# A batched weight gradient in bf16 on one core: five plain row pairs ahead of 27 combined ones, one set of sums packed into three PSUM banks, nine closing sums on GpSimd

## The chip, the core and the metric

The kernel runs on one core of a Trainium2 chip. The metric is the device time of one execution in microseconds. The kernel before takes 162.29 us, the median of three runs (162.11 to 162.46). All times inside an execution are microseconds from the start of the profiled span.

## What is computed

```python
# input: 16 x 512 x 1024 f32, grad_output: 16 x 512 x 768 f32
grad_weight = np.einsum('bmk,bmn->kn', input, grad_output)   # 1024 x 768 f32
```

Batch and row are summed over together, so this is one product X^T G with X of 8192 x 1024 and G of 8192 x 768. The products are done in bf16 with f32 sums.

## The kernel before

**Tiles.** The 8192 rows are taken as 32 pairs of 128 rows. `LOADS` (line 12) names the kind of each pair, in the order in which they are loaded: "s" is a plain pair, "P" a combined one. The output is cut into halves of K and of N, which gives four blocks: A (left K, left N), B (left K, right N), C (right K, left N) and D (right K, right N). A half of K is four groups of 128 columns, numbered q = 0 to 3. One product on TensorE is 128 rows of X by one q, times 384 columns of G.

A plain pair gives each block its two products per q: 2 x 4 x 4 = 32 products. A combined pair is treated as a two by two block matrix (its two rows by the two halves), of which seven products instead of eight are formed, as in Strassen's method: 7 x 4 = 28 products. Some of the seven work on the loaded data, others on sums of halves. VectorE makes these sums beforehand in six instructions a pair, three on X (`sum_x`, lines 179 to 187) and three on G (`sum_g`, lines 189 to 197). The seven products go to the streams A, B, C and to four more, 1, 5, 6 and 7 (`operands`, line 224). D gets products of plain pairs alone.

**Sums.** There are 32 running sums (a stream and a q), each 128 x 384 in f32, and eight PSUM banks. So most sums come and go: a bank is opened for one, gets some products, and is evicted into SBUF (`acc` for A to D, `macc` for 1, 5, 6, 7). There are two ways to take a sum up again. Either ScalarE first copies the stored part back into the bank and the products add onto it (`fill`, line 265, copy on line 274), and then the eviction is a plain copy (line 327 on ScalarE, line 329 on VectorE). Or the bank starts empty and VectorE adds bank and stored part when it evicts (line 331). The four sums of A stay in four banks of their own, 7, 3, 4 and 1, until the end; the other sums rotate through banks 0, 2, 5 and 6.

At the end the streams are put together (`close`, lines 301 to 321): 6 and 7 first get what they share (`SHARED`, line 253), 5 is closed by two subtractions (lines 307 and 309), and A, B, C and D get their partner added on VectorE (line 312). Each finished piece of the output is stored at once (line 320), the first three in two halves, nearly all on SyncE's queue.

**Order.** The order of the work on TensorE, VectorE and ScalarE is written out by hand in `PLAN` (lines 22 to 77), a list of tokens that the loop on line 336 turns into instructions. Each engine works through its own in this order. `A1@4.1` is one product for A, q = 1, in a newly opened bank 4, `A1.2` two more into the bank that is open. `f` fills a bank on ScalarE, `c` evicts on ScalarE and `v` on VectorE. `g0.6` to `g2.6` and `x0.6` to `x2.6` are the six sums of pair 6, and `r0` to `r4` round pieces of the first operands to bf16. The plan has 924 products; the last seven, of B3, are done in a 256-column and a 128-column piece each, as that sum lies in two banks there.

**Loads.** The first X and half of the first G come in f32 over the queues of SyncE and ScalarE and are rounded by VectorE and ScalarE (`round_by`, line 199). All the rest is loaded by GpSimd's queue, which converts to bf16 on the way (lines 152, 153, 157 and 159), one G and one X transfer a pair, in the order of `LOADS`. Each goes into one of 14 buffers. Until the first operands are there, TensorE runs four warm-up products (`WARMUP`, line 80): two of 512 columns in bf16 and two in f32.

Of the kernel before, what the change touches and what calls it, by code (L numbers as in the profile page):

```python
# [11 lines left out]
LOADS = "ssssssPPPPPPPPPPPPPPPPPPPPPPPPPs"  # L12

PLAN = (
    "A0@7.1 A3@3.1 A1@4.1 C3@5.1 C2@0.1 C1@2.1 r0 cC3 C0@6.1 vC2 A2@1.1 cC1 D0@5.1 vC0 B0@0.1 cD0 D1@2.1 "
    "r1 r3 B3@6.1 r2 D3@5.2 vB0 r4 A1.1 A2.1 cD1 vB3 A3.1 B1@0.2 cD3 B2@2.2 vB1 D2@6.2 cB2 C0@5.1 C1@0.1 "
    "vD2 A0.1 fD0@2 A2.1 vC0 A3.1 fD1@6 A1.1 D0.2 vC1 C2@5.2 cD0 D1.2 vC2 C3@0.2 cD1 B0@2.2 vC3 B3@5.3 "
    "fB1@6 vB0 A0.2 fB2@0 vB3 B1.2 fC0@2 B2.2 cB1 C1@5.2 vB2 C0.2 fD2@6 A3.1 vC1 D3@0.2 cC0 D2.2 fC2@5 "
    "vD3 C3@2.1 A1.1 cD2 A2.1 vC3 C2.1 B0@0.1 D1@6.1 vC2 D0@2.1 vB0 fD2@5 A3.2 vD1 A1.2 fB0@0 D2.2 vD0 "
    "B1@6.2 cD2 B0.2 vB1 B2@2.2 cB0 B3@5.2 vB2 C0@6.2 fC1@0 A2.2 vB3 fC2@2 C1.2 vC0 C3@5.2 cC1 C2.2 vC3 "
    "fD0@6 A0.2 D1@0.4 vC2 D3@5.4 vD1 D0.4 vD3 C3@2.2 vD0 B3@5.2 C0@0.2 vC3 fC1@6 A3.2 vB3 fB2@2 A0.2 vC0 "
    "C1.2 fD2@5 B2.2 cC1 D2.2 vB2 C2@0.2 cD2 B0@6.2 vC2 fB1@2 A1.4 vB0 fC1@0 B1.4 C2@5.2 cB1 D2@6.2 vC2 "  # L30
    "C1.2 fD0@2 A2.4 vD2 fD3@5 vC1 fC3@6 D0.2 D3.2 vD0 C3.2 cD3 C0@0.2 vC3 B2@2.4 vC0 fB3@6 B0@5.4 vB2 "
    "fD1@0 B3.4 fC0@2 vB0 A3.1 g0.6 fB1@5 A3.3 vB3 A0.2 g1.6 A0.2 fC1@6 D1.1 g2.6 D1.3 A2.2 vD1 A1.3 x0.6 "
    "fC2@0 C0.3 C1.1 x1.6 C1.2 cC0 C2.1 x2.6 C2.2 cC1 C3@2.1 g0.7 C3.2 cC2 B1.3 fD0@6 vC3 D2@0.2 g1.7 cB1 "
    "D0.2 vD2 fD3@2 A2.1 A3.1 A0.1 g2.7 cD0 10@5.1 D3.2 c10 x0.7 11@0.2 cD3 12@6.2 v11 13@5.2 c12 50@2.1 "
    "x1.7 50.1 c13 51@0.2 x2.7 52@6.2 c50 g0.8 53@5.2 c51 70@2.2 v52 c53 A2.1 g1.8 A3.1 fB3@0 72@6.2 v70 "
    "73@5.2 c72 g2.8 B3.2 v73 63@2.2 cB3 B2@6.1 x0.8 B2.1 fC1@5 A1.2 v63 A0.2 71@0.1 x1.8 71.2 vB2 62@2.3 "
    "c71 x2.8 C1.2 c62 g0.9 60@6.3 cC1 61@2.1 g1.9 61.2 fB0@0 v60 10@5.2 c61 g2.9 B0.3 v10 fC3@6 C2@2.2 "
    "cB0 x0.9 C2.1 C3.3 fC0@5 vC2 A2.2 f52@0 C0.1 x1.9 cC3 C0.2 A3.1 x2.9 A3.1 cC0 12@2.1 g0.10 12.1 52.2 "
    "f63@5 v12 B1@6.3 c52 g1.10 63.2 f13@2 vB1 11@0.2 c63 A0.1 g2.10 13.2 v11 72@5.2 c13 x0.10 A1.2 f51@0 "
    "53@6.2 v72 A0.1 f70@2 A3.1 51.1 x1.10 f50@5 51.2 v53 70.3 c51 x2.10 50.2 f73@6 g0.11 50.1 B3@0.3 c70 "  # L40
    "v50 73.2 fB2@2 g1.11 73.1 vB3 A2.1 f10@5 B2.2 c73 g2.11 B2.1 10.1 x0.11 10.2 cB2 C1@0.3 c10 x1.11 "
    "62@6.2 f71@2 vC1 A3.1 A1.1 f61@5 A0.1 x2.11 71.2 f60@0 g0.12 71.1 61.3 v62 c71 60.1 g1.12 60.2 c61 "
    "B0@2.1 g2.12 fB1@6 B0.2 v60 11@5.2 vB0 B1.2 fC0@0 A2.1 x0.12 A2.1 cB1 A0.1 C0.3 fC2@2 v11 A3.1 fC3@6 "
    "A1.1 x1.12 C2.3 cC0 x2.12 13@5.2 f53@0 g0.13 13.1 C3.3 cC2 v13 53.2 f52@2 g1.13 53.1 vC3 12@5.3 c53 "
    "g2.13 52.3 f72@6 v12 63@0.2 x0.13 c52 63.1 72.3 f62@5 v63 A2.1 f51@2 A1.1 x1.13 62.2 c72 51.1 x2.13 "
    "51.2 f50@0 v62 73@6.3 c51 g0.14 50.3 f70@5 v73 A3.1 fB2@2 A0.1 70.1 g1.14 c50 70.2 g2.14 B3@6.3 c70 "
    "B2.1 x0.14 B2.2 10@5.3 vB3 cB2 C1@0.1 x1.14 C1.2 f60@6 v10 11@2.3 x2.14 60.2 f61@5 g0.15 60.1 A1.1 "
    "61.3 c60 vC1 A0.1 g1.15 71@6.3 c61 v11 B0@0.1 fB1@5 g2.15 B0.2 v71 A2.2 fC2@2 A3.1 x0.15 A3.1 f52@6 "
    "B1.3 vB0 C2.2 cB1 x1.15 C2.1 52.2 cC2 x2.15 52.1 C0@0.1 fC3@5 g0.16 C0.2 A1.1 c52 A0.1 vC0 C3.3 "
    "f12@2 g1.16 13@6.3 vC3 12.2 g2.16 f62@5 12.1 v13 53@0.3 c12 x0.16 62.3 f72@6 A1.1 v53 63@2.3 c62 "  # L50
    "x1.16 f50@0 72.4 v63 f51@5 50.1 g0.17 50.2 c72 70@2.1 x2.16 70.2 c50 g1.17 51.3 v70 73@6.2 g2.17 c51 "
    "73.1 B2@0.1 x0.17 fB3@2 B2.2 A2.2 fC1@5 v73 B3.3 x1.17 C1.3 vB2 cB3 10@6.2 x2.17 cC1 10.1 71@0.1 "
    "g0.18 f11@2 71.2 A3.2 v10 f60@5 11.1 g1.18 11.2 v71 60.3 c11 g2.18 61@6.3 c60 x0.18 A0.3 fC0@2 v61 "
    "B1@0.3 fB0@5 x1.18 C0.3 fC2@6 vB1 B0.2 cC0 x2.18 B0.1 C2.1 g0.19 f12@0 C2.2 C3@2.3 cB0 vC2 12.2 "
    "f62@5 g1.19 12.1 vC3 A1.2 c12 53@6.1 g2.19 53.2 f52@2 x0.19 13@0.4 v53 A3.2 52.1 x1.19 f72@6 52.3 "
    "v13 62.2 x2.19 c52 62.2 g0.20 73@0.3 c62 g1.20 63@2.4 f51@5 v73 72.1 g2.20 72.2 fC1@0 v63 51.3 c72 "
    "x0.20 A2.3 c51 70@2.1 x1.20 70.3 f71@5 x2.20 50@6.4 v70 C1.1 g0.21 C1.2 fB2@2 A0.2 v50 cC1 B2.2 "
    "g1.21 B2.2 fB3@6 g2.21 A1.2 cB2 B3.4 x0.21 71.3 cB3 B0@0.2 x1.21 c71 B0.1 10@6.2 x2.21 10.2 vB0 "
    "C2@2.2 g0.22 C2.1 f61@0 A3.2 vC2 11@5.3 g1.22 11.1 f60@2 61.4 v10 g2.22 60.4 v11 c61 x0.22 C0@6.4 "
    "f53@0 c60 12@5.1 x1.22 12.3 vC0 B1@2.2 x2.22 B1.2 g0.23 C3@6.4 v12 53.2 g1.23 53.2 vB1 A1.2 c53 vC3 "  # L60
    "52@5.3 f73@2 g2.23 13@0.2 x0.23 13.2 A2.3 v52 A0.1 x1.23 A0.2 f51@5 v13 A3.2 51.1 x2.23 51.2 g0.24 "
    "51.1 73.3 c51 g1.24 73.1 C1@6.1 g2.24 C1.2 c73 63@5.4 vC1 f72@2 70@0.1 x0.24 f71@6 70.2 72.5 v63 v70 "
    "f62@5 A1.2 x1.24 c72 71.2 g0.25 71.2 f50@0 62.1 x2.24 fB2@2 62.2 g1.25 62.2 c71 B2.1 g2.25 B2.3 c62 "
    "50.4 vB2 B0@6.1 x0.25 f10@2 B0.3 c50 C2@5.1 x1.25 C2.3 f11@0 vB0 10.2 x2.25 10.2 g0.26 11.4 c10 vC2 "
    "B3@6.2 f60@2 g1.26 B3.2 c11 g2.26 B3.1 60.4 vB3 fB1@0 61@5.2 fC0@6 x0.26 61.2 c60 B1.4 v61 12@2.1 "
    "x1.26 fC3@5 12.3 vB1 C0.2 g0.27 f53@0 C0.2 x2.26 C3.2 cC0 g1.27 C3.2 v12 53.3 cC3 g2.27 53.1 52@6.4 "
    "v53 A2.1 x0.27 f51@0 A2.3 v52 A3.3 x1.27 A3.1 f70@6 A0.2 x2.27 A0.2 g0.28 A1.3 13@2.1 g1.28 13.2 "
    "g2.28 13.1 C1@5.4 v13 51.4 f73@2 vC1 70.1 x0.28 f63@5 70.3 c51 73.1 x1.28 73.3 c70 x2.28 73.1 63.2 "
    "c73 g0.29 63.3 f72@2 50@0.1 g1.29 50.2 c63 g2.29 50.1 71@6.4 v50 f62@5 72.4 fB0@0 v71 62.1 x0.29 "
    "f11@6 62.3 c72 B0.1 x1.29 B0.3 c62 x2.29 11.4 fB2@2 vB0 fC2@5 B2.1 g0.30 B2.4 f10@0 v11 C2.4 vB2 "  # L70
    "f11@6 10.1 g1.30 f12@2 10.3 vC2 A2.1 g2.30 A2.2 c10 x0.30 12.4 f13@5 f10@0 x1.30 11.1 13.3 c12 v11 "
    "10.1 A3.1 f61@2 x2.30 A3.2 v13 f62@6 A1.3 v10 f63@5 61.5 f60@0 62.2 v61 60.5 v62 f71@2 A2.2 f72@6 "
    "v60 A3.2 A1.2 vA2 f70@0 A0.5 vA3 vA1 70.3 vA0 63.2 v70 f50@1 71.2 72.2 fC0@3 v63 50.2 f73@0 v71 C0.6 "
    "f51@4 v72 fC1@5 v50 51.3 f52@2 fC2@7 C1.5 vC0 fD0@6 v51 fB0@1 52.4 fD1@3 B0.4 vC1 fB1@4 C2.3 v52 "
    "fD2@5 B1.7 vB0 fB2@2 vC2 73.2 vB1 B2.3 v73 f53@1 D0.2 D1.2 fC3@4 vB2 53.4 vD0 C3.6 vD1 v53 fD3@0 "
    "fB3@2+7 D2.2 D3.2 vC3 B3.7 vD2 vD3 vB3 "
).split()


WARMUP = [("b", 512), ("f", 512), ("f", 512), ("b", 512)]  # L80
PAIRS_HELD = 14
SUMS_HELD = 10

MERGED = 2


@with_exitstack
def kernel(
# [6 lines left out]
    nc = tc.nc  # L95
# [155 lines left out]


    SHARED = {"A": "1", "B": "5", "C": "7", "D": "1", "6": "1", "7": "6"}

    done = {(p, q): 0 for p in streams for q in range(Q)}
    fresh = {(p, q): True for p in streams for q in range(Q)}
    closed = set()
    opened = {}
    used = {7}
    stores = [0]  # L260

    def bank(b):
        return psum.tile([P, 512], f32, name=f"bank{b}")

    def fill(p, q, b, b2):
        assert (p, q) not in opened and not fresh[p, q] and b in used
        src = sum_of(p, q)
        if b2 is None:
            parts = [(bank(b), 0, NH)]
        else:  # L270
            assert b2 in used
            parts = [(bank(b), 0, 256), (bank(b2), 256, NH)]
        for tile_, c0, c1 in parts:
            nc.scalar.copy(out=tile_[:, 0 : c1 - c0], in_=src[:, c0:c1])  # L274
        opened[p, q] = (parts, True)

    def multiply(p, q, b, n):
        first = (p, q) not in opened
        if first:
            opened[p, q] = ([(bank(b), 0, NH)], False)  # L280
            used.add(b)
        parts, carried = opened[p, q]
        for tile_, c0, c1 in parts:
            for j in range(n):
                at = done[p, q] + j
                stat, mov = operands(p, streams[p][at], q)
                nc.tensor.matmul(  # L287
                    tile_[:, 0 : c1 - c0],
                    stat,
# [7 lines left out]
    def close(engine, p, q):  # L297
# [34 lines left out]
        if final:  # L332
            closed.add((p, q))
# [51 lines left out]
```

## Time and profile before

The profiled execution:

| what | value |
|---|---|
| time of the profiled execution | 162.31 us |
| its span | 160.5 us |
| granted TensorE clock, mean | 1.00 |
| read from HBM, written to HBM | 58.72 MB, 3.15 MB |
| GpSimd's load queue (q0) | 9360 packets, 28.64 MB, 90.2% of 16 DMA engines |
| median from issue to landing, X and G loads of a pair | 16.9 and 16.7 us |
| last load issued by GpSimd, last X landed | 125.6, 142.7 |
| first and last product start | 5.19, 156.64 |
| products of line 287, instructions | 631 on loaded data, 300 on sums |

The page gives busy time of each engine (PE is TensorE, PEld its weight loads, DVE VectorE, ACT ScalarE, POOL GpSimd, SP SyncE), the span in 40 slices with the busy share in tenths, the chain of work that ended last, and groups of instructions of one line and shape with busy time, the mean duration of one, and the idle time of the engine before them with what ended it. Instructions of one engine overlap by their fill and drain, so the mean duration of one is longer than the step from one to the next; where a step is spoken of, it is taken from the start times in the trace.

### The profile page before, as it was taken

What the parts mean: (1) busy time and instruction counts of PE and PEld (TensorE: products, weight loads), DVE (VectorE), ACT (ScalarE), POOL (GpSimd) and SP (SyncE); (2) the same over time, 40 slices, a digit from 0 to 9 for tenths busy, and PEclk for the clock granted to TensorE, in tenths of its full rate; (3) what the DMA queues carried; (4) which work ended last, traced back from release to release, by engine and by line L of the source; (5) the groups of instructions that cost most, each with busy time, mean ns of one, the idle gap of its engine ahead of it and who ended that gap; (6) DMA issues with size and microseconds to landing.
All of it is one profiled execution on the core that took longest, in us unless ns stands there. A gap on an engine that the chain in (4) does not pass through costs nothing.

```text
span 160.5 us, 2776 instructions
## 1 busy us (share of the span) xinstructions
PE 155.3 (97%) x937; PEld 91.9 (57%) x937; DVE 142.7 (89%) x323; ACT 112.8 (70%) x253; POOL 34.8 (22%) x69
## 2 busy tenths in 40 slices
PE   8899999999999999999999999999999999999990
PEld 3355556556556656655655655665665665556560
DVE  0788986989999999999989998998899998989992
ACT  3779737749888999968777786534777368877730
POOL 7452222122221222222122222212222100000000
PEclk9999999999999999999999999999999999999999
DMA  5999999999999999999999999999999999924385
GB/s 176 295 213 213 210 216 213 213 213 212 213 212 212 213 213 214 210 214 213 215 214 213 213 212 212 213 212 214 213 210 213 215 212 214 212 43 157 137 294 196
DMA packets 12830, 33.40 MB, mean 208 GB/s; under 512 B 1424, under 2 KB 4624, under 8 KB 12816
## 3 DMA queue, kind: packets, MB, share of 16 engines
q0 software_dynamic: 9360, 28.64, 90.2%
q1 hardware_dynamic: 3024, 3.47, 6.3%
q10 hardware_dynamic: 432, 1.11, 1.8%
q8 instruction: 7, 0.11, 0.3%
q14 instruction: 7, 0.06, 0.1%
HBM read 58.72 MB, written 3.15 MB: 385 GB/s over the span
## 4 chain that ended last, share of the span: by engine, by line
DMA 48%; PE 44%; DVE 2%; issue 2%; POOL 1%; DVEq 0%; POOLq 0%
DMA xp<-in_input_dram 48%; PE bank L287 44%; POOL gp L157 1%; DVE acc L312 1%; DVE xe L183 0%; POOL xp L159 0%; DVE acc L331 0%; DVE macc L331 0%; DVEq L380 0%; DVE xe L185 0%; POOLq L153 0%; POOLq L369 0%; POOLq L152 0%
## 5 line engine op out<-in xcount | busy, mean ns | idle before, releaser
L287 PE MATMUL bank<-gp,xp 128*128 128x384 bf16 (+2 forms) x631 | 109.8, 324 | 0.6 <-DVE xp L201 0.6
L287 PEld LDWEIGHTS <-xp 128*128 128x128 bf16 x631 | 61.1, 98 | 42.5 <-DVE xp L201 1.3
L287 PE MATMUL bank<-ge,xe 128*128 128x384 bf16 x300 | 56.2, 326 | 0.1
L274 ACT COPY bank<-macc 128x384 f32<-128x384 f32 x71 | 33.6, 484 | 13.2 <-DVE macc L331 5.6
L287 PEld LDWEIGHTS <-xe 128*128 128x128 bf16 x300 | 29.3, 98 | 19.9 <-issue 0.6
L274 ACT COPY bank<-acc 128x384 f32<-128x384 f32 (+1 forms) x70 | 32.3, 479 | 9.1 <-DVE acc L329 5.5
L327 ACT COPY macc<-bank 128x384 f32<-128x384 f32 x61 | 28.6, 479 | 9.5 <-PE bank L287 8.1
L331 DVE TENSOR_TENSOR acc<-bank,acc 128x384 f32<-128x384 f32 x54 | 28.7, 552 | 2.8 <-PE bank L287 1.2
L153 POOL DMA_DIRECT2D xp<-in_input_dram x30 | 16.0, 532 | 53.3 <-DMA xp<-in_input_dram 28.0
L327 ACT COPY acc<-bank 128x384 f32<-128x384 f32 x45 | 21.4, 480 | 6.5 <-PE bank L287 6.0
L152 POOL DMA_DIRECT2D gp<-in_grad_output_dram x30 | 16.0, 533 | 37.1 <-DMA gp<-in_grad_output_dram 15.0
L331 DVE TENSOR_TENSOR macc<-bank,macc 128x384 f32<-128x384 f32 x41 | 22.5, 551 | 0.5 <-PE bank L287 0.2
L183 DVE TENSOR_TENSOR xe<-xp 128x1024 bf16<-128x1024 bf16 x25 | 17.1, 683 | 1.2 <-DMA xp<-in_input_dram 1.2
L329 DVE COPY acc<-bank 128x384 f32<-128x384 f32 x24 | 13.1, 553 | 3.0 <-PE bank L287 2.4
L193 DVE TENSOR_TENSOR ge<-gp 128x768 bf16<-128x768 bf16 x25 | 13.8, 550 | 0.0
L187 DVE TENSOR_TENSOR xp<-xp,xe 128x512 bf16<-128x512 bf16 x25 | 10.5, 419 | 0.4
L185 DVE TENSOR_TENSOR xe<-xe,xp 128x512 bf16<-128x512 bf16 x25 | 10.5, 418 | 0.3
L197 DVE TENSOR_TENSOR gp<-ge,gp 128x384 bf16<-128x384 bf16 x25 | 8.8, 352 | 0.3
L195 DVE TENSOR_TENSOR ge<-gp,ge 128x384 bf16<-128x384 bf16 x25 | 8.7, 350 | 0.2
L312 DVE TENSOR_TENSOR acc<-bank,macc 128x384 f32<-128x384 f32 (+2 forms) x17 | 8.0, 522 | 0.0
L329 DVE COPY macc<-bank 128x384 f32<-128x384 f32 x14 | 7.6, 552 | 0.4 <-PE bank L287 0.4
L201 DVE CAST gp<-gf 128x192 bf16<-128x192 f32 (+1 forms) x2 | 0.7, 360 | 4.9 <-DMA gf<-in_grad_output_dram 4.9
(17 smaller groups left out, 21.6 us busy)
## 6 DMA issues: line engine op xcount, KB each, us to landing
xp<-in_input_dram POOLq DMA_DIRECT2D x30, 512.0 KB, 16.9
gp<-in_grad_output_dram POOLq DMA_DIRECT2D x30, 384.0 KB, 16.7
out_dram<-acc SPq DMA_DIRECT2D x12, 192.0 KB, 1.9
xf<-in_input_dram ACTq DMA_DIRECT2D x2, 512.0 KB, 5.0
gp<-in_grad_output_dram POOLq DMA_DIRECT2D x3, 192.0 KB, 6.6
out_dram<-acc SPq DMA_DIRECT2D x6, 96.0 KB, 1.7
xp<-in_input_dram POOLq DMA_DIRECT2D x2, 256.0 KB, 8.0
gf<-in_grad_output_dram SPq DMA_DIRECT2D x2, 192.0 KB, 4.2
```

Of the source, the lines that this page charges most:

```text
L152: nc.gpsimd.dma_start(out=gp, in_=G[rows, :].rearrange("(p m) n -> p m n", m=2))
L153: nc.gpsimd.dma_start(out=xp, in_=X[rows, :].rearrange("(p m) k -> p m k", m=2))
L183: nc.vector.tensor_sub(out=xe[:, 0:2, :], in0=x[:, 1::-1, :], in1=x[:, 3::-2, :])
L185: nc.vector.tensor_sub(out=xe[:, 2, :], in0=xe[:, 0, :], in1=x[:, 0, :])
L187: nc.vector.tensor_add(out=x[:, 1, :], in0=x[:, 2, :], in1=xe[:, 2, :])
L193: nc.vector.tensor_add(out=ge[:, 0:2, :], in0=g[:, 0:2, :], in1=g[:, 1::2, :])
L274: nc.scalar.copy(out=tile_[:, 0 : c1 - c0], in_=src[:, c0:c1])
L287: nc.tensor.matmul(tile_[:, 0 : c1 - c0], stat, mov[:, c0:c1], start=first and j == 0, stop=True, skip_group_check=True,)
L312: nc.vector.tensor_add(out=dst[:, c0:c1], in0=b, in1=sum_of(SHARED[p], q)[:, c0:c1])
L327: nc.scalar.copy(out=dst, in_=b)
L329: nc.vector.tensor_copy(out=dst, in_=b)
L331: nc.vector.tensor_add(out=dst, in0=b, in1=dst)
```

## The change

Seven things are changed together.

- `LOADS`: the first five pairs are plain and the other 27 combined. Before, six were plain at the start and one at the end. So there are 916 products.
- A's four sums lie packed in three banks, 5, 6 and 7. The sums of q = 0 and 3 lie whole in bank 5 and bank 7; those of q = 1 and 2 lie across two banks, 128 columns in one and 256 in the other, so that each of their products is done in two pieces, each with its own weight load. Five banks, 0 to 4, rotate for the other streams.
- D, which ends with the plain pairs, is folded into C by an addition and into 7 by a subtraction when one of their banks is evicted (token `k`, on VectorE). At the end D is 5 less the finished 7, without an addition of its own.
- A may be evicted, and B and C may be closed, by a ScalarE copy, and GpSimd then adds the shared part in SBUF (`add_shared`). Token `q` adds and stores (seven times), token `p` adds beforehand, so that the last eviction is a plain copy or an addition (twice).
- `PLAN` is written anew.
- The warm-up is one bf16 product of 512 columns and 32 of 128 columns.
- The first four stores go out in halves (`HALVED`), and the last two, of B0 and B1, use ScalarE's queue (suffix `a`).

```diff
-LOADS = "ssssssPPPPPPPPPPPPPPPPPPPPPPPPPs"
+LOADS = "sssssPPPPPPPPPPPPPPPPPPPPPPPPPPP"
 PLAN = (
-    "A0@7.1 A3@3.1 A1@4.1 C3@5.1 C2@0.1 C1@2.1 r0 cC3 C0@6.1 vC2 A2@1.1 cC1 D0@5.1 vC0 B0@0.1 cD0 D1@2.1 "
...
-    "fD2@5 B1.7 vB0 fB2@2 vC2 73.2 vB1 B2.3 v73 f53@1 D0.2 D1.2 fC3@4 vB2 53.4 vD0 C3.6 vD1 v53 fD3@0 "
-    "fB3@2+7 D2.2 D3.2 vC3 B3.7 vD2 vD3 vB3 "
+    "A0@R.1 A1@R.1 C1@0.1 C0@1.1 C3@2.1 cC1 C2@3.1 r0 A2@R.1 cC0 vC3 D1@4.1 B0@0.1 cC2 A3@R.1 vD1 B1@1.1 "
...
+    "51.2 pC0 fB3@0 51.1 71.1 C1.1 v50 C1.1 fB0@5 C1.1 A3.2 qC3 fB2@1 A3.2 v71 cC1 A3.1 B3.2 f52@4 vA3 B3.2 "
+    "qC1 fB1@6 B3.1 v51 C0@2.2 cB3 52.2 B2.2 vC0 qB3 B2.2 B0.1 v52 B0.1 cB2 B0.3 qB2 B1.2 vB0a B1.2 vB1a "
 ).split()
-WARMUP = [("b", 512), ("f", 512), ("f", 512), ("b", 512)]
+WARMUP = [("b", 512)] + 32 * [("b", 128)]
+HALVED = 4
-    SHARED = {"A": "1", "B": "5", "C": "7", "D": "1", "6": "1", "7": "6"}
+    SHARED = {"A": "1", "B": "5", "C": "7", "6": "1", "7": "6"}
+    def resident_parts(q):
+        if not resident:
+            resident.update({b: bank(b) for b in (5, 6, 7)})
+        a, b, c = (resident[i] for i in (5, 6, 7))
+        return [
+            [(a, 0, 0, NH)],
+            [(a, NH, 0, 128), (b, 0, 128, NH)],
+            [(b, 256, 0, 256), (c, 0, 256, NH)],
+            [(c, 128, 0, NH)],
+        ][q]
+        for tile_, at, c0, c1 in parts:
+            b = tile_[:, at : at + c1 - c0]
+            to = dst[:, c0:c1]
+            if engine == "c":
+                nc.scalar.copy(out=to, in_=b)
+            elif engine == "k":
+                d = sum_of("D", q)[:, c0:c1]
+                (nc.vector.tensor_add if p == "C" else nc.vector.tensor_sub)(out=to, in0=b, in1=d)
+            elif final and p == "5":
+                nc.vector.tensor_sub(out=to, in0=b, in1=sum_of("6", q)[:, c0:c1])
+                d = sum_of("D", q)[:, c0:c1]
+                nc.vector.tensor_sub(out=d, in0=b, in1=sum_of("7", q)[:, c0:c1])
+                store("D", q, c0, c1, queue)
+    def add_shared(p, q, prepare, queue):
+        dst = sum_of(p, q)
+        nc.gpsimd.tensor_add(out=dst, in0=dst, in1=sum_of(SHARED[p], q))
+        if prepare:
+            prepared.add((p, q))
+        else:
+            closed.add((p, q))
+            store(p, q, 0, NH, queue)
```

## The prediction

> **What bounds the kernel now.** I read the page from the top: busy shares, then the slices, then the chain, then the groups of instructions.
>
> ```profile
> PE 155.3 (97%) x937; PEld 91.9 (57%) x937; DVE 142.7 (89%) x323; ACT 112.8 (70%) x253; POOL 34.8 (22%) x69
> ...
> DMA  5999999999999999999999999999999999924385
> ...
> DMA xp<-in_input_dram 48%; PE bank L287 44%; POOL gp L157 1%; DVE acc L312 1%; DVE xe L183 0%; POOL xp L159 0%; DVE acc L331 0%; DVE macc L331 0%; DVEq L380 0%; DVE xe L185 0%; POOLq L153 0%; POOLq L369 0%; POOLq L152 0%
> ```
>
> Two things run at their limit side by side. TensorE is busy for 97%, and the loads fill the DMA engines up to slice 35 of 40, about 140 us; the chain is shared between them, 48 to 44. VectorE (89%) is next, ScalarE (70%) has room. Is TensorE really full where it is "busy"? The table by stretch says so, and shows how the two evicting engines stand there (columns: stretch, its length, then busy time and instructions of PE, PEld, DVE, ACT, POOL, then clock, DMA share, GB/s):
>
> ```profile
> 40.00:50.00 10.00, 10.00 (x64) 6.03 (x62) 9.86 (x24) 8.60 (x21) 2.65 (x5) 1.00 1.06 212
> 50.00:60.00 10.00, 10.00 (x63) 6.00 (x62) 9.92 (x25) 9.25 (x22) 2.12 (x4) 1.00 1.07 212
> ...
> 100.00:110.00 10.00, 10.00 (x64) 6.05 (x62) 9.88 (x24) 4.37 (x10) 2.38 (x5) 1.00 1.07 213
> ```
>
> TensorE takes some 62 products in 10 us at the full clock, and the start times of the trace give a step of 0.1625 us for 384 columns, 0.109 for 256, 0.056 for 128. VectorE works 99% of 40 to 60 us and TensorE loses nothing by it: a planned order can run an evicting engine full.
>
> So the path is: first product at 5.19 us (it waits for the rounded first operands), 917 whole products and 7 in two pieces: 917 x 0.1625 + 7 x (0.109 + 0.056) = 150.17, and 0.16 for the last to drain: 155.52. TensorE ends at 156.86, so it stood for 1.3 in all (0.5 in the first 2.6 us of products, 0.3 at 14 to 17, 0.3 at 84, 0.1 at 142 us, the last three at places where a load lands). Behind that stand the last sums and stores:
>
> ```profile
> 156.78 0.61 DVE L312 TENSOR_TENSOR acc<-bank,macc 128x256 f32<-128x256 f32 x2
> 156.89 0.87 SPq L320 DMA_DIRECT2D out_dram<-acc  x2
> 157.42 0.36 ACTq L320 DMA_DIRECT2D out_dram<-acc  x1
> ```
>
> VectorE ends at 157.39, 0.53 behind TensorE; the store and the end take the rest of the 160.5. This execution took 162.31, 1.8 more than its span, and the median of the runs is 162.29, so no correction is needed.
>
> **Part by part.**
>
> *Five plain pairs for seven.* A plain pair is 32 products, a combined one 28: 2 x 4 = 8 products less, 924 to 916. A's sums 1 and 2 now lie across two banks, so their 37 products each become a 128-column and a 256-column piece: 842 x 0.1625 + 74 x (0.056 + 0.109) = 149.04. Against 150.17: **-1.13 us**, on the path. Two more pairs need their sums, six DVE instructions each; from the start times one pair costs 0.60 + 0.33 + 0.34 + 0.48 + 0.27 + 0.29 = 2.3 us, together +4.6.
>
> *A in three banks.* Five banks rotate instead of four. The orders spend this on ScalarE: counted from the two lists of tokens,
>
> - ScalarE: copies out 106 to 146, fills 140 to 191 (141 with the split one). Its rows:
>
> ```profile
> L274 ACT COPY bank<-macc 128x384 f32<-128x384 f32 x71 | 33.6, 484 | 13.2 <-DVE macc L331 5.6
> ...
> L327 ACT COPY macc<-bank 128x384 f32<-128x384 f32 x61 | 28.6, 479 | 9.5 <-PE bank L287 8.1
> L331 DVE TENSOR_TENSOR acc<-bank,acc 128x384 f32<-128x384 f32 x54 | 28.7, 552 | 2.8 <-PE bank L287 1.2
> ```
>
>  The 480 ns overlap: the next one starts 0.376 after a copy out and 0.417 after a fill (medians; means of unbroken pairs 0.402 and 0.429).
> - VectorE: 166 evictions to 144 (132, eight that fold D in, four second halves of 5). At a step of 0.469: -10.3, and +4.6 for the sums: 5.7 us less. It isn't the end now and isn't then.
>
> The stretch that decides is product 62 to 682 (15 to 116 us), 620 x 0.1625 = 100.75 us of TensorE. There ScalarE gets 138 fills and 106 copies out (now 88 and 81). At the medians 138 x 0.417 + 106 x 0.376 = 97.4; at the means 138 x 0.429 + 106 x 0.402 = 101.8; its longer unbroken runs step at 0.400 to 0.427, mean 0.412, so 244 x 0.412 = 100.5. ScalarE goes from 70% to full. The cost on TensorE is between 0 (97.4 fits) and 101.8 - 100.75 = 1.1; I take **0.6**, the middle, since a queue that is never empty should come nearer to its medians than today's, whose steps hold short waits. What speaks for little is VectorE above, full without a stall, and the fifth bank, which gives each fill more time.
>
> *D folded into C and 7.* Eight additions of 0.469 on VectorE in mid-kernel replace four at the end; counted above. They hide under products; uncovered they would cost 3.8.
>
> *New orders and the loads.* The loads themselves stay: same order and sizes, Pool issues, queue of some 17 us between issue and landing. So each lands when it does today, and TensorE can't be ahead of that. First use against landing: the input of pair 19 is read by product 521, 5.19 + 520 x 0.1625 + 0.1 of pieces = 89.8, and lands at 90.6: 0.8 of standing is forced. The last pair lands at 142.7, its first sum takes 0.6, and product 846 (142.7 by the step) reads it: 0.7, the same 0.8 in effect. I take 0.8 for the loads plus 0.6 for ScalarE: **1.4** of standing, against 1.3 today. The bounds are 0.8 and 0.8 + 1.1 + 0.8 = 2.7, the last 0.8 for the first ten us (22 ScalarE copies and 5 roundings in them, some 9.1 + 1.8 against 10.1).
>
> *Short warm-up.* Today's ends at 4.63, before the operands are there (5.09). 33 short ones, at twice the warm step of 0.056 while the clock is low, take 0.38 + 32 x 0.112 = 4.0 from 0.78: 4.7. Hidden; above 5.19 each 0.1 would cost 0.1.
>
> *GpSimd's nine sums, the end.* They start after product 848, when Pool has issued its last load (125.6) long ago; what waits behind one on Pool is the next sum, on SP the stores queued after it. No row shows an addition on Pool: the bounds are 0.53 (a DMA issue on Pool, L153) and 2.2 (four times the VectorE row of 0.55). The last, B2, waits for a copy out 9 products before the end: start 0.9 before TensorE ends, so it may take 1.6 before its store (1.9 to land) ends later than that of B1 (0.03 + 0.55 on VectorE, 2.1 to land). I take about 0.9, nearest to the VectorE row: hidden; at 2.2, +0.6. The Trainium skill (GPSIMD Engine Reference, section 3) calls GpSimd the wrong engine for plain elementwise work, 4497 ns where VectorE needs 2293 for 2048 elements; scaled to 384 that is an estimate of 0.84, and the sum would be the same.
>  The end of VectorE is 0.58 behind TensorE where it was 0.53: **+0.05**.
>
> **Sum.** -1.13 + (1.4 - 1.3) + 0.05 = -0.98: 162.31 - 0.98 = **161.3 us**.
>
> **Rivals.**
>
> 1. *ScalarE becomes the bound (slower).* If it steps not at 0.41 but at 0.42, the busy time per instruction of 50 to 60 us (9.25 / 22), the stretch takes 244 x 0.42 = 102.5, 1.75 over. With 0.8 for the first ten us and 0.8 from the loads, standing is 3.35, +2.05: 162.31 - 1.13 + 2.05 + 0.05 = **163.3**. It decides from standing of 2.4, a step of about 0.416 with the start's 0.8 in it. For it: 244 copies in 100 us where the densest 10 us today hold 22. Against it: the medians. Chance 0.25.
> 2. *The clock comes late.* The rows give the full clock from 3.93 us, 3.15 behind the first warm-up product. If the short ones didn't count as work, the first real ones would run at half rate for as long and lose 1.6, of which the forced 0.8 takes a part: 0.8 to 1.0 more than forecast, **162.2**, no difference. Against it: 32 in a row leave hardly a gap. Chance 0.08.
> 3. *Weight loads show.* A 128-column piece streams for 0.056 but its weight load takes 98 ns by the page (L287, PEld). If it weren't hidden, 74 x (0.098 - 0.056) = 3.1 is lost and the time is **164.4**. Against it: seven such pieces in a row at the end step at 0.056, each with its own load. The Trainium skill (TensorE: Matmul & The Clock Gate, "Back-to-back issue gap") gives about 81 ns a product for streams of 128 columns with weight loads; by that 74 x 0.025 = 1.9 would be lost, and the trace disagrees with its 0.056. Chance 0.04.
> 4. *It doesn't do what it says at the end*: a slow Pool keeps the last store, +0.6, **161.9**. Chance 0.05.
>
> The forecast (160.7 to 161.9) has 0.58. Of it 0.55 is faster and 0.03 no difference. Rival 1: 0.23 slower, 0.02 no difference. Rival 2: 0.02, 0.05, 0.01. Rival 3: 0.04 slower. Rival 4: 0.03 and 0.02. With what only the loads hold back (standing of 0.8, 160.7), no better time has much chance. That makes 0.60 faster, 0.12 within 0.2% (0.32 us, about what a measurement of this kernel can tell from no change), 0.28 slower. The range runs from 160.5, a little under the loads' bound, to 163.5, which holds rival 1's price and leaves out its upper part and rival 3.
>
> **What would show it.** 916 blocks in 990 instructions of line "PE MATMUL bank", 128-column steps of 0.056; ScalarE above 90% with 337 copies and steps of 0.40 to 0.41; standing of TensorE near 1.4, most of it where loads land; TensorE's end near 155.8; Pool's additions near 0.9 and over before the last store. If ScalarE has no idle stretch from 15 to 116 us and TensorE waits for fills (L274's successor), rival 1 holds. Wrong would be the sum above all if ScalarE's step under load isn't the one between today's medians and means.

## The result, and the profile after

The changed kernel takes 164.43 us (164.33 to 164.53, four runs) against 162.38 of the kernel before on the same chip: a ratio of 1.0126 (95% interval 1.0105 to 1.0147). It is 1.3% slower; forecast was 161.3, with a range that ended at 163.5.

The page of the changed kernel, the lines that answer to those shown before: busy shares, the DMA slices, the chain, and the groups of ScalarE's fills and copies.

```profile
PE 154.1 (95%) x1023; PEld 96.5 (59%) x1023; DVE 139.8 (86%) x313; ACT 142.1 (87%) x345; POOL 43.6 (27%) x78
...
DMA  5999999999999999999999999999999999802693
...
PE 81%; DMA 12%; DVE 2%; issue 1%; DVEq 0%; POOLq 0%
...
L301 ACT COPY bank<-macc 128x384 f32<-128x384 f32 x106 | 49.9, 498 | 1.6 <-DVE macc L357 0.5
L301 ACT COPY bank<-acc 128x384 f32<-128x384 f32 x85 | 40.9, 500 | 1.8 <-DVE acc L357 1.0
```

TensorE works for 1.2 us less, ScalarE for 29 more, and the chain is now TensorE's for 81%. Nothing there says why the whole is longer. The DMA digits give a first hint: after the loads there is a hole (8, 0, 2) and then a nearly full stretch (6, 9) before the last slice. The same by stretches, last columns DMA share and GB/s; the first two fences are of the changed kernel, the third has the kernel before in the first stretch behind the loads:

```profile
15.00:116.00 101.00, 100.71 (x668) 62.78 (x667) 93.88 (x215) 98.51 (x244) 24.32 (x46) 1.00 1.07 213
```
```profile
142.00:149.00 7.00, 6.86 (x47) 4.27 (x46) 6.29 (x12) 5.95 (x16) 2.70 (x3) 1.00 0.09 29
149.00:153.00 4.00, 4.00 (x27) 2.40 (x25) 4.00 (x10) 3.83 (x10) 3.21 (x5) 1.00 0.41 127
153.00:157.00 4.00, 3.19 (x20) 1.71 (x18) 3.70 (x8) 1.48 (x4) 2.97 (x3) 1.00 0.96 338
```
```profile
142.00:149.00 7.00, 7.00 (x44) 4.13 (x43) 6.72 (x15) 5.31 (x13) 0.00 (x0) 1.00 0.35 115
```

From 15 to 116 us the change does what it was to do: ScalarE is busy 98.5 of 101 us, and TensorE for all but 0.3 of them. Behind the loads, the stores hardly run until 149 us (29 GB/s; the kernel before moved 115 there) and fill the DMA engines from 153 to 157 (96%, 338 GB/s).

The page ends its chain with the last work. What comes behind it is found among the instructions that close the program: the group of GpSimd's drains (count, then min, median and longest in ns, then first and last start), first in the kernel before, then in the changed kernel, and the last additions of the changed kernel.

```profile
L380 POOLq DRAIN  x3: 45/99/19803, 125.6 to 160.3; - x3
```
```profile
L424 POOLq DRAIN  x3: 45/93/6427, 155.3 to 162.3; - x3
```
```profile
154.08 1.00 POOL L369 TENSOR_TENSOR acc<-acc,macc 128x384 f32<-128x384 f32 x1
155.38 1.00 POOL L369 TENSOR_TENSOR acc<-acc,macc 128x384 f32<-128x384 f32 x1 [0.30 <-ACT acc L339]
```

The long drain begins at 155.3, beside the last addition (155.38 to 156.38), and ends at 161.77, 5.39 behind it and 1.1 behind SyncE's first closing drain (160.64), which comes behind the last store. In the kernel before it begins behind GpSimd's last load and is over at 145.41, long before the end. Where the 2.0 us of span come from, by points that the trace gives for both kernels:

| point, us | before | after | nine sums left out (e1) |
|---|---|---|---|
| last product ends | 156.86 | 156.20 | 155.86 |
| last VectorE sum ends | 157.39 | 156.85 | 156.51 |
| last store lands | 159.57 | 160.49 | 158.85 |
| GpSimd's long drain ends | 145.41 | 161.77 | 145.49 |
| span | 160.54 | 162.56 | 159.75 |

The computing ends 0.55 earlier. The last store lands 3.64 behind it, where it was 2.18: +1.46. The end of the span lies 2.07 behind the last landing, where it was 0.97: +1.10. Together -0.55 + 1.46 + 1.10 = +2.01. These are differences of points in time, not prices: the drain runs beside the stores, so what each of the two costs by itself has to come from experiments.

### The profile page after: what moved, and what is told of

Its sections match the earlier page's. It is cut to its first block, busy times and chain, and to the rows that moved or that the text cites. A ratio compares the mean times of both kernels' runs of the same rounds, so it can differ in the third digit from the quotient of the medians.

```text
span 162.6 us, 3054 instructions
## 1 busy us (share of the span) xinstructions
PE 154.1 (95%) x1023; PEld 96.5 (59%) x1023; DVE 139.8 (86%) x313; ACT 142.1 (87%) x345; POOL 43.6 (27%) x78
## 4 chain that ended last, share of the span: by engine, by line
PE 81%; DMA 12%; DVE 2%; issue 1%; DVEq 0%; POOLq 0%
PE bank L320 81%; DMA xp<-in_input_dram 8%; DMA gp<-in_grad_output_dram 4%; DVE xp L190 0%; DVE acc L353 0%; DVE macc L357 0%; DVE macc L353 0%; DVE xe L188 0%; DVEq L353 0%; POOLq L413 0%
## 5 line engine op out<-in xcount | busy, mean ns | idle before, releaser
L320 PE MATMUL bank<-gp,xp 128*128 128x384 bf16 (+2 forms) x666 | 106.8, 308 | 1.3 <-DVE xp L204 0.8
L320 PE MATMUL bank<-ge,xe 128*128 128x384 bf16 x324 | 61.7, 326 | 0.0
L301 ACT COPY bank<-macc 128x384 f32<-128x384 f32 x106 | 49.9, 498 | 1.6 <-DVE macc L357 0.5
L301 ACT COPY bank<-acc 128x384 f32<-128x384 f32 x85 | 40.9, 500 | 1.8 <-DVE acc L357 1.0
L339 ACT COPY acc<-bank 128x384 f32<-128x384 f32 (+2 forms) x71 | 33.3, 482 | 5.1 <-PE bank L320 4.7
L339 ACT COPY macc<-bank 128x384 f32<-128x384 f32 x77 | 35.9, 503 | 1.3 <-PE bank L320 0.9
L156 POOL DMA_DIRECT2D xp<-in_input_dram x30 | 15.9, 530 | 51.8 <-DMA xp<-in_input_dram 23.5
L359 DVE TENSOR_TENSOR acc<-bank,acc 128x384 f32<-128x384 f32 x42 | 21.8, 549 | 0.6 <-PE bank L320 0.2
L357 DVE COPY macc<-bank 128x384 f32<-128x384 f32 x29 | 15.9, 553 | 2.4 <-PE bank L320 2.0
L369 POOL TENSOR_TENSOR acc<-acc,macc 128x384 f32<-128x384 f32 x9 | 8.9, 1006 | 21.1 <-ACT acc L339 18.4
L359 DVE TENSOR_TENSOR macc<-bank,macc 128x384 f32<-128x384 f32 x21 | 11.3, 547 | 0.0
```

The lines of the kernel that those rows point to most:

```text
L156: nc.gpsimd.dma_start(out=xp, in_=X[rows, :].rearrange("(p m) k -> p m k", m=2))
L301: nc.scalar.copy(out=tile_[:, at : at + c1 - c0], in_=src[:, c0:c1])
L320: nc.tensor.matmul(tile_[:, at : at + c1 - c0], stat, mov[:, c0:c1], start=fresh, stop=True, skip_group_check=True,)
L339: nc.scalar.copy(out=to, in_=b)
L357: nc.vector.tensor_copy(out=to, in_=b)
L359: nc.vector.tensor_add(out=to, in0=b, in1=to)
```

## The experiments

The theory was "GpSimd's end": both losses come from the nine additions, by the drain that closes GpSimd behind them and by the stores that wait for them. The first rival was "the stores", late because the new order finishes the output late.

**e1: the nine additions left out**, so the stored pieces lack their shared part.

```diff
-        nc.gpsimd.tensor_add(out=dst, in0=dst, in1=sum_of(SHARED[p], q))
```

> The changed kernel with GpSimd's nine additions left out (the stored pieces lack their shared part). Theory, 'GpSimd's end': what makes the change slower sits behind its additions alone: GpSimd's closing drain, which ends 5.4 us after its last addition (156.4 to 161.8), and SyncE's stores, which stand in a row behind the sums. Without them the drain ends near 145 as in the kernel before, the stores start 3 us earlier, the last lands near 159.2, and the time falls from 164.4 to 161.7 (161.3 to 162.1). Rival, 'stores': the late stores alone set the end, because the new order finishes the output later; then the last still lands after 160 and the time stays above 163.

161.63 us, ratio 0.9961 (0.9948 to 0.9974): the rest of the change is worth 0.7 us. The drain is over at 145.5, with the loads, the first stores go out 1.3 us earlier and the second piece 3.3 (it is A1 there, whose copy ends first; in the changed kernel it is A0), and the last lands at 158.85. The theory holds; the additions cost 2.8 us.

**e2: one late addition in the kernel before.**

```diff
+            if token == "vC3" and "vC3" not in PLAN[at + 1 :]:
+                src = sum_of("C", 3)
+                nc.gpsimd.tensor_add(out=spare, in0=src, in1=src)
```

> The kernel before with one GpSimd addition of 128x384 f32 into a spare tile, ready when C3 is closed (near 155.9 us), that nobody waits for. Theory, 'GpSimd's end': it runs from 156.0 to 157.0, the drain behind it ends 5.4 us later at 162.4, and the time rises by 2.6 us to 164.9. Rival, 'stores': nothing waits for this addition, so the time stays within 0.3 of 162.3.

165.07, ratio 1.0167 (1.0152 to 1.0182). The only addition on GpSimd, and the closing behind it, of this kernel:

```profile
155.99 0.82 POOL L352 TENSOR_TENSOR spare<-acc 128x384 f32<-128x384 f32 x1 [29.56 <-DVE acc L313]
```
```profile
L384 POOLq DRAIN  x3: 45/93/6259, 155.9 to 162.7; - x3
```

It ends at 156.81 and the drain at 162.21, again 5.39 later. The last store lands at 159.55 as ever. One addition that nobody waits for costs 2.7 us.

**e3: the same addition early.**

```diff
+            if token == "x2.29":
+                src = sum_of("D", 0)
+                nc.gpsimd.tensor_add(out=spare, in0=src, in1=src)
```

> The kernel before with the same addition right behind GpSimd's last load issue, near 126 us. Theory, 'GpSimd's end': the drain still waits for the loads (145.4 in the kernel before) and is over long before the end, so the time stays within 0.3 of 162.3. Rival, 'any arithmetic on GpSimd makes the closing longer, wherever it stands': 1 us or more on top, 163.3.

162.35, ratio 1.0008 (0.9996 to 1.0020). It runs at 126.5, and the drain ends at 145.3 behind the loads, as without it. So it isn't arithmetic on GpSimd that costs, but how late it comes.

**e4: whole stores only** in the changed kernel.

```diff
-HALVED = 4
+HALVED = 0
```

> The changed kernel with whole stores only (no store in halves), which takes 4 issues of 0.4 to 0.5 us off SyncE's queue, which issues without a pause from 149.7 to 157.5. Theory, 'GpSimd's end': the last store lands up to 1 us earlier, but the drain of GpSimd ends at 161.8 as before, so the time stays within 0.3 of 164.4. Rival, 'stores': the time falls with the last landing, by 0.7 to 1.2 us to 163.5.

164.63, ratio 1.0138 (1.0121 to 1.0155). The time stays, as the theory had it, but not by the way it named: the last landing didn't become earlier either (160.57). In this execution TensorE stood 0.43 longer in the first 30 us than in that of the changed kernel, and what comes behind it is nearly as much later; from one execution to the next this part varies (1.1 to 1.6 us of standing with the same order). Counted from VectorE's end the last store did land earlier, by 0.3 (3.34 behind it, against 3.64).

**e6: the sums written aside**, into a spare tile, so that no store waits for them (the stored pieces lack their shared part).

```diff
-        nc.gpsimd.tensor_add(out=dst, in0=dst, in1=sum_of(SHARED[p], q))
+        nc.gpsimd.tensor_add(out=spare, in0=dst, in1=sum_of(SHARED[p], q))
```

> The changed kernel with GpSimd's nine additions written into a spare tile, so that no store waits for them (the stored pieces lack their shared part). They run where they ran. This parts the two costs. Theory, 'GpSimd's end': the stores are as early as without the additions, the last landing near 158.9, yet the drain still ends 5.4 us behind the last addition near 161.7, and the time is 164.3, as with the change. Rival, 'the stores that stand behind the sums are what costs': 161.7 to 162.3.

164.50, ratio 1.0145 (1.0127 to 1.0164). The last store lands at 159.23, 1.3 earlier than with the change, and the time is the same: the drain alone (156.53 to 161.92) holds it.

**e5: the last two sums on VectorE**, all computed.

```diff
-C0@2.2 cB3 52.2 B2.2 vC0 qB3 B2.2 B0.1 v52 B0.1 cB2 B0.3 qB2 B1.2 vB0a
+C0@2.2 vB3 52.2 B2.2 vC0 B2.2 B0.1 v52 B0.1 vB2 B0.3 B1.2 vB0a
```

> The changed kernel with B3 and B2 closed by VectorE (one addition each straight from the bank) instead of by a ScalarE copy and a GpSimd addition; all is computed. GpSimd's last addition is then that of C1, near 154.0. Theory, 'GpSimd's end': its drain ends 5.4 us later at 159.4 and no longer decides; VectorE has two additions of 0.47 more and ends near 157.5, the last store lands 2.5 us later near 160.1, and the time is 162.9 (162.4 to 163.4), 1.5 under the changed kernel. Rival, 'VectorE pays': it is so full at the end that the two additions come back in full and the stores are as late as before, 163.8 or more.

163.38, ratio 1.0072 (1.0050 to 1.0095). GpSimd's last addition ends at 154.14, its drain at 159.54, and the span follows the last store now (160.78). So with the drain out of the way the late stores still keep this version slower than the kernel before. Not all of that is the sums' doing: VectorE ends at 157.64, 0.8 later than in the changed kernel, since it had hardly any room for the two. An estimate for the changed kernel's own stores without the drain: its last landing at 160.49, then 0.97 to the end of the span and 1.77 behind it as in the kernel before, make 163.2, 0.8 slower. The drain alone costs the whole loss (e6).

**e11: a memset in place of the late addition** of e2.

```diff
+                nc.gpsimd.memset(sum_of("7", 3), 0.0)
```

> The kernel before with one GpSimd memset of 128x384 f32 near 156 us, where the late addition was (it clears a part of macc that is no longer read). Theory, 'the drain waits 5.4 us behind any computing instruction of GpSimd': drain near 162.0, 164.7. Rival, 'it is the addition, or its two inputs': the drain is over before the stores, 162.3.

164.37, ratio 1.0122 (1.0107 to 1.0136). The memset takes 0.42 and ends at 156.48, the drain at 161.88: 5.39 behind it once more. So the drain comes as late behind either of the two computing instructions; it isn't the addition.

**e9: the first sum moved.** In the changed kernel VectorE's last sum on X (the second line) runs beside GpSimd's first addition (the third):

```profile
144.31 0.41 DVE L188 TENSOR_TENSOR xe<-xe,xp 128x512 bf16<-128x512 bf16 x1
144.75 1.10 DVE L190 TENSOR_TENSOR xp<-xp,xe 128x512 bf16<-128x512 bf16 x1
```
```profile
144.54 1.03 POOL L369 TENSOR_TENSOR acc<-acc,macc 128x384 f32<-128x384 f32 x1 [18.13 <-ACT acc L339]
```

```diff
-cA2 63.1 73.1 63.1 x1.31 13.1 f72@1 qA2 13.1 A1.1 x2.31 62.1 c13 63.1 72.1 v62 cA1
+63.1 73.1 63.1 x1.31 13.1 f72@1 13.1 A1.1 x2.31 62.1 c13 63.1 72.1 v62 cA2 qA2 cA1
```

> The changed kernel with GpSimd's first sum (A2) moved behind the last sum on X of the last pair. In the changed kernel the two run beside each other and that sum takes VectorE 1.10 us, against 0.43 without GpSimd's additions. Theory, 'GpSimd holds VectorE where both read two inputs from SBUF': the sum takes 0.43 again, TensorE ends 0.3 us earlier (155.9), and with it GpSimd's last addition and its drain: 164.1. Rival, 'the slow one has another cause' (the load just landed): it stays at 1.1 us, 164.4.

164.56, ratio 1.0128 (1.0111 to 1.0145). The sum, in e9:

```profile
145.10 0.43 DVE L190 TENSOR_TENSOR xp<-xp,xe 128x512 bf16<-128x512 bf16 x1
```

It takes 0.43 again, so the overlap with GpSimd was its cause. But TensorE gained nothing by it: from 140 us on it stands 0.43 (0.37 in the changed kernel), so the second half of the expectation fell. The traces name other waits. In the changed kernel a product at 146.4 us waits 0.31 for a VectorE eviction that stood behind the slow sum. In e9 two products, at 146.5 and 147.2, wait 0.26 and 0.18 for ScalarE, for a copy and a fill that stand right behind the two copies of A2, and the edit had moved these there. e1 has neither the slow sum nor the move, and TensorE doesn't stand there.

**e7: the short warm-up alone** in the kernel before.

```diff
-WARMUP = [("b", 512), ("f", 512), ("f", 512), ("b", 512)]
+WARMUP = [("b", 512)] + 32 * [("b", 128)]
```

> The kernel before with the short warm-up alone. Theory, 'hidden': the first product starts within 0.1 us of 5.2 and the time stays within 0.3 of 162.3. Rival, 'the clock comes late': first products at half rate, 1 us more.

162.49, ratio 1.0011 (1.0001 to 1.0022). The first product starts at 5.19 as before, and the time stays within 0.3: hidden, or nearly so, as the interval begins just above 1. The rival isn't quite gone. In this execution the full clock comes at 5.34 us (3.93 in the kernel before, 3.80 in the changed kernel); up to it the 128-column products of the warm-up step at 0.107, twice the 0.056 of later ones. It comes behind the start of the first product, which loses 0.06. Of the ten traces with the short warm-up six have the full clock only behind the first product (5.34 to 6.59); the four with the long one have it between 3.48 and 4.97. These are too few to blame the warm-up. In e10, where it comes at 6.35, the first products lose 0.5, yet TensorE's standing in the first 30 us is 1.18 against 1.12 in the changed kernel, as it then waits less for the loads at 16 and 21 us (0.26 against 0.61).

**e8: twelve more ScalarE copies** in the changed kernel.

```diff
+            if op == "g" and int(stage) == 0 and 10 <= int(u) < 22:
+                nc.scalar.copy(out=spare, in_=sum_of("D", 0))
```

> The changed kernel with 12 more ScalarE copies of 128x384 f32 from SBUF to SBUF, spread from 49 to 100 us, where it is busy for 49.5 of 50 us. Theory, 'ScalarE is at its bound in the changed kernel, only just': 12 x 0.38 = 4.6 us of work against some 1 to 2.5 us of slack; TensorE falls behind by 2 to 4 us and the time is 166.4 to 168.4. Rival, 'ScalarE only looks full, since its copies wait in the fill': the time stays within 0.5 of 164.4.

168.46, ratio 1.0388 (1.0360 to 1.0417). Its stretch from 45 to 105 us, where TensorE and ScalarE of the changed kernel are busy 60.00 and 59.36:

```profile
45.00:105.00 60.00, 58.90 (x373) 35.16 (x371) 56.04 (x130) 59.90 (x150) 14.78 (x28) 1.00 1.07 213
```

TensorE's standing between 30 and 140 us goes from 0.26 to 3.86, and the time comes out just above the range expected. The step that follows one of the twelve copies is 0.41 in this trace, together 5.0 us, so 5.0 - 3.6 = 1.4 was about all the room that ScalarE had.

**e10: mended**, all computed: e5 and e9 together, whole stores, and the last seven stores on the two queues in turn.

```diff
-"qC1 fB1@6 B3.1 v51 C0@2.2 cB3 52.2 B2.2 vC0 qB3 B2.2 B0.1 v52 B0.1 cB2 B0.3 qB2 B1.2 vB0a B1.2 vB1a "
+"qC1 fB1@6 B3.1 v51a C0@2.2 vB3 52.2 B2.2 vC0a B2.2 B0.1 v52 B0.1 vB2a B0.3 B1.2 vB0 B1.2 vB1a "
```

> All is computed. The changed kernel with what the runs before showed: B3 and B2 closed by VectorE, the first sum moved as in the run beside it, whole stores, and the last seven stores taken by the queues of SyncE and ScalarE in turn. Theory, 'three costs at the end': GpSimd's last addition ends near 154.0, its drain near 159.4; VectorE ends near 157.0, 0.6 under the run with two sums on VectorE, and the last store lands near 159.3: 162.1 (161.7 to 162.6), no longer slower than the kernel before. Rival, 'VectorE has no room at the end': it ends at 157.6 as in that run, and the time is 162.8 or more.

163.13, ratio 1.0047 (1.0034 to 1.0060): 1.3 us better than the change and still slower than the kernel before. The drain ends at 159.39 and decides nothing. VectorE ends at 157.54, as the rival said, and the last store lands 2.6 behind that, at 160.17.

**e12: one sum less on VectorE** in that version (the part of the edit in `PLAN`, against e10; a further line stores C0 behind its ScalarE copy).

```diff
-fB1@6 B3.1 v51a C0@2.2 vB3 52.2 B2.2 vC0a
+fC0@2 fB1@6 B3.1 v51a C0.2 vB3 52.2 B2.2 cC0
```

> All is computed. The mended version with C0's last stretch taken up by a ScalarE fill and closed by a ScalarE copy (its shared part was added beforehand), so that VectorE, which works there without a pause from 149 us to its end at 157.5, has one addition of 0.47 less. Theory, 'VectorE sets the end of the mended version': it ends near 157.1, the last store lands near 159.7, the time falls by 0.4 to 162.7 (162.4 to 162.9). Rival, 'the stores set it': the last landing stays within 0.15 of 160.2 and the time at 163.1.

163.21, ratio 1.0052 (1.0034 to 1.0070). VectorE ends 0.23 earlier (157.31) though TensorE ends 0.31 later here, and the last store doesn't follow: 160.28. The rival holds: in the mended versions the row of stores sets the end. e10 by stretches shows it:

```profile
142.00:149.00 7.00, 6.89 (x47) 4.20 (x46) 5.87 (x12) 5.65 (x16) 2.79 (x3) 1.00 0.08 29
149.00:153.00 4.00, 4.00 (x27) 2.42 (x25) 4.00 (x10) 3.84 (x10) 3.09 (x5) 1.00 0.43 152
153.00:157.00 4.00, 3.34 (x21) 1.78 (x19) 4.00 (x10) 0.59 (x2) 1.00 (x1) 1.00 0.96 343
```

Until 149 us it stores no more than the changed kernel, and from 153 on the DMA engines are full. None of these versions that compute everything is faster than the kernel before.

## Why the prediction was wrong, step by step

- **Five plain pairs, pieces of A: right.** The trace has 990 product instructions, 74 of 128 and 74 of 256 columns, with steps of 0.056 and 0.109. The forecast of TensorE's end was 155.8; it is 156.20, and 155.86 in e1.
- **Standing of 1.4: nearly right, its parts not.** It is 1.76: 1.12 in the first 30 us, 0.26 from 30 to 140 us and 0.37 behind that. For the loads I took 0.8, forced by one that lands at 90.6; 0.61 is lost at two that land at 16.3 and 21.2, and no wait is left at 90. For ScalarE I took 0.6; by the start times the products between 15 and 116 us wait 0.16 for it (at 15.9 and 53.0). The steps came out below today's medians, 0.371 after a copy and 0.413 after a fill: 138 x 0.413 + 106 x 0.371 = 96.3. Rival 1 had the place right (e8: 1.4 us of room), and it didn't decide.
- **Short warm-up, D folded in: right as far as seen.** The first product starts at 5.24 for 5.19, and e7 is 0.2 longer by the medians; rival 2's late full clock does show in some executions. Of the second nothing is seen in the standing.
- **Weight loads (rival 3): not seen.** The 74 pieces of 128 columns, each with a load of its own, step at 0.056.
- **The end: this step failed.** It said of GpSimd's additions "hidden" and added +0.05. The additions take 1.0, near the 0.9 assumed, and VectorE ends 0.65 behind TensorE, near the 0.58. Three things were missing. First, the drain: 5.39 us behind the last addition, where the step looked only at who waits for the sum. It is the bound of the changed kernel, at 161.77. Second, what stands in line. The second sum in GpSimd's queue, for C2, waits for VectorE until 147.33. The one for A0, whose copy and whose part of stream 1 are both there at 147.72, starts behind it at 148.29 and ends at 149.30; SyncE's next store waits for A0 until then, and all others behind that, A1 too, whose copy was over at 145.95. I named these queues and priced none; with the stores freed from the sums the last one lands 1.26 earlier (e6). Third, the landing times of 1.9 and 2.1 came from a kernel whose stores were spread; here 18 go out from 149.3 on, the last two with 3.1 and 3.4 to land.
- **Rival 4** ("it doesn't do what it says at the end") named the right place with 0.6 us and a chance of 0.05. The additions cost 2.8 (164.43 against 161.63).

Without the additions the sum stands: 162.31 - 1.13 + 0.10 + 0.05 gave 161.3, e1 gives 161.6. That it comes so near is in part luck, as the standing in e1 (1.38) is the forecast one while its parts are not.

## What to carry to other kernels

Look at what closes the program, too: an instruction on an engine that was idle at the end can hold the whole by its drain, and costs nothing if it is early enough (e2 and e3 are the same addition). Work that stores wait for belongs to the end as much as the last sum: price each queue behind the first that waits. Putting the sums in the order in which they are ready would be the next thing to try; no run here did. And a landing time is that of its crowd: 1.7 to 2.1 us for spread stores, 3.4 at the end of a row that fills the DMA engines.

## What the runs showed of the hardware

- GpSimd's drain ends 5.39 us behind its last computing instruction, in all ten runs that had a late one (5.394 or 5.395, an addition or a memset; one, seven or nine of them). Behind loads alone it ended 2.7 behind the last landing (142.71 to 145.41). What it does in that time the trace doesn't show.
- A VectorE sum of two bf16 inputs from SBUF took 1.10 beside a GpSimd addition, 0.43 without (e9). The Trainium skill (GPSIMD Engine Reference, section 1) has GpSimd share its SBUF interfaces with VectorE and names instructions with two SBUF inputs; the trace agrees. VectorE's additions of a bank and an SBUF tile kept their 0.54 beside GpSimd's.
- ScalarE's step is 0.37 for 128x384 f32 out of a bank and 0.41 into one, in a stretch in which it was busy for 98.5 of 101 us.
